# Weights that stream through the array stand 80 bytes nearer to the front of their ring places than weights that are loaded into it

## The chip, the cores and the metric

The kernel runs on one core of one Trainium2 chip. The metric is the device time of one execution in microseconds (us). TensorE (PE in the rows, PEld for its weight loads) multiplies, ScalarE (ACT) and VectorE (DVE) work elementwise, and SyncE (SP) issues the DMAs. GpSimd does nothing here.

## The reference, cut to what matters

Two layers of a decoder trunk on 256 tokens of width 2048, all in float32: a gated linear recurrence, then an attention with three branches, each followed by an MLP of width 8192 with a squared ReLU. Every sub-layer is shifted, scaled and gated by vectors that come from a condition vector and a large matrix (`ada_w`).

```
for layer in range(DEPTH):
    ...
    h = x * (1.0 + scale[:, 0, None]) + shift[:, 0, None]
    if mixer == 0: y = rglru_mixer(h, ...)      # h @ w_in, conv, gates, scan, (...) @ w_out
    elif mixer == 1: y = nsa_mixer(h, ...)      # h @ w_in, three attentions, (...) @ w_out
    x = _layer_norm(DN_ALPHA * x + (1.0 + gate[:, 0, None]) * y, ...)
    h = x * (1.0 + scale[:, 1, None]) + shift[:, 1, None]
    y = (jnp.square(jax.nn.relu(h @ w1)) @ w2)
    x = _layer_norm(DN_ALPHA * x + (1.0 + gate[:, 1, None]) * y, ...)
```

Nearly all the arithmetic is in the large products with `w_in`, `w_out`, `w1` and `w2`.

## The kernel before

**Three matmuls for one product.** A float32 operand is split into a rounded part (hi, type fp32r) and the rest (lo). `mm3` (L193 to L197) makes a product from three matmuls that add up in one PSUM bank: hi by hi (L195), hi by lo (L196), lo by hi (L197).

**The ring.** All large weights go through one stream. SP loads a unit of 128x2048 into one of six `raw` buffers (L104), ACT writes its rounded half to `whi` (L137) and DVE the rest to `wlo` (L138), 1024 columns at a time, that is two pieces of 512. `whi` and `wlo` are rings of 16 pieces; piece i lies in place i % 16, 2048 bytes a place. `pump` writes a pair of pieces only if the pair has room behind the piece that is being used (L132), and `take` (L185) moves that mark by one. The same `pump` runs the `ada` units, each a pass of DVE over 128x2048 (L120).

**Two ways to multiply.** In `gemm_ws` and `gemm_ws_outer` (L199 to L226) the weights are loaded into the array: four slices of 128 columns of a piece are loaded in turn, and 256 columns of the activations (tiles `s`) move through, so a piece takes twelve matmuls of 256 columns. In `gemm_as` (L228 to L259) a slice of 128 columns of the activations is loaded, and the whole piece of 512 columns moves through, for two halves of the tokens: six matmuls of 512 columns a piece. Rows name the moving operand last in one case and first in the other: `g<-s,whi` is a matmul of the first kind, with shape 128x256, and `g<-whi,s` one of the second, with shape 128x512.

The second kind is used for `lru_out`, for all `mlp_w2`, for two units of columns of `nsa_kv`, for `nsa_out`, and for the first 512 columns of `mlp_w1` in layer 1: 43 products of 16 pieces. Everything else is of the first kind. In the built program `whi`, `wlo` and all `s` tiles begin at multiples of 64 bytes in each partition, and so does every piece and every slice.

**The order** is that of a recorder's clock (`now`), with guessed durations (L205 to L257); the chip's own times don't enter it.

Of the kernel before, what the change touches and what calls it, by code (L numbers as in the profile page):

```python
# [10 lines left out]
F32R = mybir.dt.float32r  # L11
# [18 lines left out]

RAW = 6
RING = 16
NS4 = 20
NS2 = 6
LNACT = (0, 2)
# [5 lines left out]
class Item:  # L41
    def __init__(self, kind, src, col=None, then=None, width=2048):
        self.kind, self.src, self.col, self.then, self.width = kind, src, col, then, width
        self.group = 0
        self.done = False
        self.run = None
        self.pieces = {"w": width // 512, "g": 2}.get(kind, 0)


class Builder:  # L50
    def __init__(self, ctx, tc, a, out):
        self.tc, self.nc, self.a, self.out = tc, tc.nc, a, out
        nc = self.nc
        self.const = ctx.enter_context(tc.tile_pool(name="const", bufs=1))
        self.pool = ctx.enter_context(tc.tile_pool(name="work", bufs=1))
        self.psum = ctx.enter_context(tc.tile_pool(name="psum", bufs=1, space=PSUM))
        self.dram = ctx.enter_context(tc.tile_pool(name="dram", bufs=1, space=DRAM))
        self.raw = self.const.tile([128, RAW, 2048], F32, name="raw")
        self.whi = self.const.tile([128, RING, 512], F32R, name="whi")
        self.wlo = self.const.tile([128, RING, 512], F32R, name="wlo")  # L60
        self.now = 0.0
        self.tasks = []
        self.items = []
        self.di = self.pi = 0
        self.cons = self.prod = 0
        self.slot = self.inflight = 0
        self.arrive = []
        self.uid = 0


    def t4(self, shape, dtype=F32):
        self.uid += 1
        return self.pool.tile(shape, dtype, name=f"s{self.uid}", tag="s4", bufs=NS4)

# [11 lines left out]

    def set_stream(self, items):
        self.items = items
        p = 0
        for it in items:  # L90
            it.p0 = p
            p += it.pieces
        self.prefetch()

    def prefetch(self):
# [13 lines left out]
    def pump(self):  # L109
        nc = self.nc  # L110
        while self.pi < len(self.items):
            it = self.items[self.pi]
            if it.kind == "d":
                self.pi += 1
                continue
            if self.arrive[self.pi] > self.now:
                return
            r = it.raw
            if it.kind == "a":
                nc.vector.scalar_tensor_tensor(r, r, self.one, self.cond, op0=OP.mult, op1=OP.mult, accum_out=it.col)  # L120
            elif it.kind == "raw":
                if not it.run(r):
                    return
            elif it.kind == "p":
                it.run(r)
            elif it.kind == "n":
                if not it.done:
                    return
            else:
                w = min(1024, it.width)  # L130
                s = it.p0 + 2 * it.group
                if s + 2 > self.cons + RING:  # L132
                    return
                src = r[:, 1024 * it.group:1024 * it.group + w]
                hi = self.whi[:, s % RING:s % RING + 2, :].rearrange("p a b -> p (a b)")[:, :w]
                lo = self.wlo[:, s % RING:s % RING + 2, :].rearrange("p a b -> p (a b)")[:, :w]
                nc.scalar.activation(hi, src, AF.Copy)  # L137
                nc.vector.tensor_tensor(out=lo, in0=src, in1=hi.bitcast(F32), op=OP.subtract)  # L138
                self.prod = s + 2
                it.group += 1  # L140
                if 2 * it.group < it.pieces:
                    continue
            self.pi += 1
            self.inflight -= 1
            self.prefetch()
            if it.then:
                it.then()
# [32 lines left out]

    def piece(self, i):
        self.until(lambda: self.prod > i)
        return self.whi[:, i % RING, :], self.wlo[:, i % RING, :]

    def take(self):  # L185
        self.cons += 1

    def head(self, kind):

        self.until(lambda: self.items[self.pi].kind == kind and not self.items[self.pi].done and self.arrive[self.pi] <= self.now)  # L190
        return self.items[self.pi], self.items[self.pi].raw
# [88 lines left out]
def build(ctx, tc, a, out):  # L280
    B = Builder(ctx, tc, a, out)
# [57 lines left out]
    def W(name, *ix):  # L339
        return Item("w", a[name][ix])  # L340

    def N(name, *ix):
        return Item("n", a[name][ix])

    def merge(main, side):
        res, j = [], 0
        for i, m in enumerate(main):
            res.append(m)
            while j < len(side) and (j + 1) * len(main) <= (i + 1) * len(side):
                res.append(side[j])  # L350
                j += 1
        return res + side[j:]
# [3 lines left out]
    def hook(key):  # L356
        return lambda: hooks[key]()
# [52 lines left out]
    lru_in = [N("lru_gate", 0), N("lru_gate", 1)]  # L410
    for c in (2, 3):
        lru_in += [W("lru_in", 4 + c, g) for g in range(4)] + [W("lru_in", c, g) for g in range(4)] + [N("lru_gate", c)]
    lru_out = [W("lru_out", n, g) for n in range(4) for g in range(4)]
    def ss_group(k0, k1):
        ks = range(k0, k1)
        return ada_items(1, 0, ks) + ada_items(1, 1, ks, hook(("h1", k0, k1)))
# [9 lines left out]
    def mlp_items(l):  # L426
        its = []
        for q in range(4):
            its += [W("mlp_w1", l, 4 * q + i, g) for i in range(4) for g in range(4)]
            its += [W("mlp_w2", l, n, 4 * q + g) for n in range(4) for g in range(4)]  # L430
        return its

    m0 = mlp_items(0)
    stream += merge(m0[16:], ada_items(1, 2, then=hook(("gate", 1))) + ada_items(2, 0) + ada_items(2, 1, then=hook(("ss", 2))) + ada_items(2, 2, then=hook(("gate", 2))))
    nsa = []
    for ch in (4, 5, 0, 1, 2, 3):
        if ch == 4 or ch == 5:
            idx = {4: 3, 5: 5}[ch]
        else:
            idx = (0, 1, 2, 4)[ch]  # L440
        nsa += [W("nsa_kv", idx, g) for g in range(4)]
# [5 lines left out]
    nsa += q_items + [W("nsa_out", n, g) for n in range(4) for g in range(4)]  # L447
# [596 lines left out]
    gbank = B.bank([128, 256], "g")  # L1044
    whi, wlo = B.piece(B.cons)
    B.until(lambda: B.prod > B.cons + 1)
    ghi = B.whi[:, B.cons % RING:B.cons % RING + 2, :].rearrange("p a b -> p (a b)")
    glo = B.wlo[:, B.cons % RING:B.cons % RING + 2, :].rearrange("p a b -> p (a b)")
# [226 lines left out]
```

## Time and profile before

| | |
|---|---|
| median of 3 runs | 2256.97 us (2256.06 to 2257.09) |
| the profiled execution | 2264.49 us |
| its span, first to last instruction | 2262.7 us |
| mean granted clock of TensorE in it | 0.988 |
| PE busy | 2166.2 us (96%) |
| DVE busy | 1637.4 us (72%) |
| ACT busy | 1058.3 us (47%) |

All rows below are from the profiled execution; 1.8 us of it lie outside the span. A matmul's duration in the trace is longer than the distance to the next one, since matmuls overlap: what a matmul costs in a dense stretch is the distance from start to start, which is the length of the stretch over the count.

### The profile page before, as it was taken

The page shows a single profiled execution, that of the slowest core. Times are in us where ns is not written, and L with a number is a line of the kernel's source. Part 1 is how long each engine was busy: PE and PEld are TensorE (multiplying, and loading weights), DVE is VectorE, ACT ScalarE, POOL GpSimd, SP SyncE. Part 2 cuts the span into 40 slices and gives each one's busy share as a digit, 9 for nine tenths or more (in the row PEclk, how much of TensorE's full clock was granted, in tenths as well). Part 3 has the DMA queues.
Part 4 walks back from the last instruction along what each step waited for, and adds up shares of the span by engine and source line. Part 5 has one row for each costly group of instructions (what it writes and reads, how often), then busy time and mean ns, then how long its engine had stood idle before and what let it go on. Part 6 is the DMA issues. An engine that isn't in the chain of part 4 may idle for free.

```text
span 2262.7 us, 34098 instructions
## 1 busy us (share of the span) xinstructions
PE 2166.2 (96%) x14089; PEld 1938.8 (86%) x14089; DVE 1637.4 (72%) x1958; ACT 1058.3 (47%) x1385; POOL 0.2 (0%) x4
## 2 busy tenths in 40 slices
PE   3799998999999999999999999999999999999997
PEld 3788877998998998998789988788989989988986
DVE  8898788897777777678887688668766454454566
ACT  2356564554453454454453355536544444543541
POOL 0000000000000000000000000000000000000000
PEclk9899999999999999999999999999999999999999
DMA  9988878699878887889689875356788555555670
GB/s 392 413 328 339 348 297 344 264 355 384 334 300 307 293 326 292 302 309 341 234 298 356 301 270 214 132 200 216 284 303 320 197 186 186 189 192 196 211 255 37
DMA packets 98775, 625.02 MB, mean 276 GB/s; under 512 B 10963, under 2 KB 13443, under 8 KB 27452
## 3 DMA queue, kind: packets, MB, share of 16 engines
q1 hardware_dynamic: 98620, 622.85, 73.6%
q8 instruction: 110, 1.80, 0.3%
q14 instruction: 45, 0.37, 0.0%
HBM read 614.36 MB, written 8.45 MB: 275 GB/s over the span
## 4 chain that ended last, share of the span: by engine, by line
PE 86%; DVE 8%; ACT 3%; issue 2%; DMA 2%; SPq 0%; DVEq 0%; ACTq 0%
PE g L196 26%; PE g L195 26%; PE g L197 26%; DVE raw L120 3%; DVE wlo L138 2%; DMA raw<-in_lru_in 1%; ACT whi L137 1%; PE m L1157 1%; PE m L1123 1%; PE m L962 1%; PE m L1149 0%; PE g L873 0%; PE m L1160 0%; PE m L379 0%; DMA raw<-in_ada 0%
## 5 line engine op out<-in xcount | busy, mean ns | idle before, releaser
L138 DVE TENSOR_TENSOR wlo<-raw,whi 128x1024 fp32r<-128x1024 f32 x721 | 870.7, 1221 | 466.7 <-ACT whi L137 465.5
L137 ACT ACTIVATE whi<-raw 128x1024 fp32r<-128x1024 f32 x721 | 754.6, 1057 | 866.0 <-PE g L197 423.7
L195 PE MATMUL g<-s,whi 128*128 128x256 f32 (+1 forms) x2768 | 776.2, 281 | 58.6 <-ACT s L529 57.6
L196 PE MATMUL g<-s,whi 128*128 128x256 f32 (+1 forms) x2768 | 774.4, 280 | 3.2 <-DVE s L530 3.2
L197 PE MATMUL g<-s,wlo 128*128 128x256 f32 (+1 forms) x2768 | 773.0, 280 | 2.3 <-DVE wlo L138 2.3
L195 PEld LDWEIGHTS g<-s,whi 128*128 128x128 f32 (+1 forms) x2768 | 522.4, 189 | 72.4 <-ACT s L529 58.6
L195 PE MATMUL g<-whi,s 128*128 128x512 f32 x1376 | 542.5, 395 | 7.6 <-ACT s L529 4.2
L196 PE MATMUL g<-wlo,s 128*128 128x512 f32 x1376 | 542.1, 394 | 1.6 <-DVE wlo L138 1.6
L197 PE MATMUL g<-whi,s 128*128 128x512 f32 x1376 | 540.6, 393 | 0.3 <-DVE s L530 0.3
L197 PEld LDWEIGHTS g<-s,wlo 128*128 128x128 f32 (+1 forms) x2768 | 525.8, 190 | 6.4 <-DVE wlo L138 4.6
L196 PEld LDWEIGHTS g<-s,whi 128*128 128x128 f32 (+1 forms) x2768 | 523.2, 189 | 6.7 <-DVE s L530 4.7
L120 DVE SCALAR_TENSOR_TENSOR raw<-raw,one,cond 128x2048 f32<-128x2048 f32 x176 | 411.4, 2346 | 34.2 <-DMA raw<-in_ada 33.3
L195 PEld LDWEIGHTS g<-whi,s 128*128 128x128 f32 x1376 | 259.4, 189 | 68.0 <-ACT s L529 5.9
L196 PEld LDWEIGHTS g<-wlo,s 128*128 128x128 f32 x1376 | 259.6, 189 | 59.4 <-DVE wlo L138 2.3
L197 PEld LDWEIGHTS g<-whi,s 128*128 128x128 f32 x1376 | 259.5, 189 | 57.9 <-DVE s L530 1.8
L195 PE MATMUL m<-s,whi 128*128 128x256 f32 x256 | 70.4, 276 | 0.2 <-ACT whi L137 0.2
L197 PE MATMUL m<-s,wlo 128*128 128x256 f32 x256 | 70.6, 276 | 0.0
L196 PE MATMUL m<-s,whi 128*128 128x256 f32 x256 | 70.6, 276 | 0.0
L488 ACT ACTIVATE s<-s,hB,hA 128x256 f32<-128x256 f32 x32 | 16.7, 592 | 100.7 <-DVE hA L464 75.2
L530 DVE TENSOR_TENSOR s<-t,s 128x512 fp32r<-128x512 f32 x78 | 53.2, 684 | 4.0 <-ACT s L529 3.8
L708 ACT ACTIVATE t<-g 128x512 f32<-128x512 f32 x58 | 34.0, 587 | 34.0 <-PE g L197 34.0
L195 PEld LDWEIGHTS m<-s,whi 128*128 128x128 f32 x256 | 47.9, 188 | 0.4 <-ACT whi L137 0.4
(192 smaller groups left out, 1058.3 us busy)
## 6 DMA issues: line engine op xcount, KB each, us to landing
raw<-in_mlp_w SPq DMA_DIRECT2D x256, 1024.0 KB, 5.1
raw<-in_ada SPq DMA_DIRECT2D x176, 1024.0 KB, 7.0
raw<-in_lru_in SPq DMA_DIRECT2D x28, 1024.0 KB, 6.1
raw<-in_nsa_kv SPq DMA_DIRECT2D x24, 1024.0 KB, 5.3
raw<-in_gate SPq DMA_DIRECT2D x16, 1024.0 KB, 10.2
raw<-in_lru_out SPq DMA_DIRECT2D x16, 1024.0 KB, 7.0
raw<-in_nsa_q SPq DMA_DIRECT2D x16, 1024.0 KB, 6.6
raw<-in_nsa_out SPq DMA_DIRECT2D x16, 1024.0 KB, 4.7
```

The costliest lines, as they stand in the source:

```text
L120: nc.vector.scalar_tensor_tensor(r, r, self.one, self.cond, op0=OP.mult, op1=OP.mult, accum_out=it.col)
L137: nc.scalar.activation(hi, src, AF.Copy)
L138: nc.vector.tensor_tensor(out=lo, in0=src, in1=hi.bitcast(F32), op=OP.subtract)
L195: mm(out, lhi, rhi, start=start, stop=False, skip_group_check=True)
L196: mm(out, lhi, rlo, start=False, stop=False, skip_group_check=True)
L197: mm(out, llo, rhi, start=False, stop=stop, skip_group_check=True)
L488: SC.activation(x[:, j, :], x[:, j, :], AF.Identity, scale=hA[s][:, k:k + 1], bias=hB[s][:, k:k + 1])
L530: V.tensor_tensor(out=lo, in0=src, in1=hi.bitcast(F32), op=OP.subtract)
L708: SC.activation(r2, banks[b], AF.Relu)
L962: T.matmul(hv, r[:, 128 * l:128 * l + 128], x[:, :, h:15 + h, l], start=(h == 0 and l == 0), stop=(h == 1 and l == 15))
L1123: T.matmul(ps, qT[:, h, 128 * t:128 * t + 128], kT[g // 2][:, g % 2, :, 0:K], start=True, stop=True)
L1157: T.matmul(po, vt[br][:, kt, 128 * g:128 * g + 128], pT[:, br, kt], start=first, stop=False)
```

## The change

Pieces get an offset within their places: 64 elements (256 bytes) where they are loaded into the array, 44 elements (176 bytes) where they move through it. Both rings grow by 64 elements. A moving pair therefore reaches into the last 20 elements of the place ahead of it. Where a unit of moving pieces follows one of loaded pieces, two places of the ring are skipped; where a loaded pair would end on the first 20 elements of a moving piece that is still in use, `pump` waits for it. The units of the second kind are marked by `moving`.

```diff
+OFF_WS, OFF_AS = 64, 44
...
-        self.whi = self.const.tile([128, RING, 512], F32R, name="whi")
-        self.wlo = self.const.tile([128, RING, 512], F32R, name="wlo")
+        self.whi = self.const.tile([128, 512 * RING + 64], F32R, name="whi")
+        self.wlo = self.const.tile([128, 512 * RING + 64], F32R, name="wlo")
...
+        self.skip, self.off = set(), {}
...
+        p, last = 0, False
         for it in items:
+            if it.pieces and it.moving and not last:
+                self.skip |= {p, p + 1}
+                p += 2
             it.p0 = p
-            p += it.pieces
+            for _ in range(it.pieces):
+                self.off[p] = OFF_AS if it.moving else OFF_WS
+                p += 1
+            if it.pieces:
+                last = it.moving
...
                 if s + 2 > self.cons + RING:
                     return
+                old = s + 2 - RING
+                if not it.moving and old >= self.cons and self.off.get(old) == OFF_AS:
+                    return
...
+                o = self.off[s] + 512 * (s % RING)
+                hi, lo = self.whi[:, o:o + w], self.wlo[:, o:o + w]
...
     def take(self):
         self.cons += 1
+        while self.cons in self.skip:
+            self.cons += 1
```

In the built program the loaded pieces still begin at multiples of 64 bytes, as do the `s` tiles. The moving pieces begin 48 bytes past such a multiple.

The matmuls, their shapes and their number stay as they are. What moves is where ACT's and DVE's conversions stand among the other work, by one or two pairs. One such place is in the first layer's MLP, at the end of the second quarter of `mlp_w1`, where the ring goes over from loaded pieces to moving ones (near 650 us). `s_5347` and `s_5571` are rounded tiles of the hidden layer, `t_` their ReLUs, `g_` PSUM banks. ACT before:

```order
L137 ACTIVATE whi<-raw 128x1024 x6
L708 ACTIVATE t_5349<-g_5098 128x512
L709 ACTIVATE t_5349<-t_5349 128x512
L137 ACTIVATE whi<-raw 128x1024
L529 ACTIVATE s_5347<-t_5349 128x512
L708 ACTIVATE t_5368<-g_5099 128x512
L709 ACTIVATE t_5368<-t_5368 128x512
L137 ACTIVATE whi<-raw 128x1024
L529 ACTIVATE s_5347<-t_5368 128x512
```

And ACT at the same place after the change (lines are numbered anew: L159 is the conversion, L557 the rounding, L736 and L737 the ReLU and the square):

```order
L159 ACTIVATE whi<-raw 128x1024 x6
L736 ACTIVATE t_5349<-g_5098 128x512
L737 ACTIVATE t_5349<-t_5349 128x512
L159 ACTIVATE whi<-raw 128x1024
L557 ACTIVATE s_5347<-t_5349 128x512
L736 ACTIVATE t_5366<-g_5099 128x512
L737 ACTIVATE t_5366<-t_5366 128x512
L557 ACTIVATE s_5347<-t_5366 128x512
```

The conversion that stood ahead of the last rounding has moved behind it: the first moving pair is written one pair later. The other place is on PE, a product of `mlp_w2` in layer 0 where two output blocks of moving pieces overlap (`g_4114` and `g_4115` are the two token halves of one block, `g_4261` and `g_4262` those of the next). PE before:

```order
L195 MATMUL g_4261<-whi,s_3906 128x512
L196 MATMUL g_4261<-wlo,s_3906 128x512
L197 MATMUL g_4261<-whi,s_3907 128x512
L195 MATMUL g_4262<-whi,s_3906 128x512
L195 MATMUL g_4114<-whi,s_3983 128x512
L196 MATMUL g_4114<-wlo,s_3983 128x512
```

And after, at the same place:

```order
L220 MATMUL g_4261<-whi,s_3906 128x512
L220 MATMUL g_4262<-whi,s_3906 128x512
L221 MATMUL g_4261<-wlo,s_3906 128x512
L222 MATMUL g_4261<-whi,s_3907 128x512
L220 MATMUL g_4114<-whi,s_3983 128x512
L221 MATMUL g_4114<-wlo,s_3983 128x512
```

The same matmuls stand there, one of them two rows earlier.

## Rows read from the trace of the kernel before

**Rows 1.** The page, busy time: engine, us, share of the span, instructions.

```profile
PE 2166.2 (96%) x14089; PEld 1938.8 (86%) x14089; DVE 1637.4 (72%) x1958; ACT 1058.3 (47%) x1385; POOL 0.2 (0%) x4
```

**Rows 2.** The page, chain of work that ended last, by engine and line.

```profile
PE 86%; DVE 8%; ACT 3%; issue 2%; DMA 2%; SPq 0%; DVEq 0%; ACTq 0%
PE g L196 26%; PE g L195 26%; PE g L197 26%; DVE raw L120 3%; DVE wlo L138 2%; DMA raw<-in_lru_in 1%; ACT whi L137 1%; PE m L1157 1%; PE m L1123 1%; PE m L962 1%; PE m L1149 0%; PE g L873 0%; PE m L1160 0%; PE m L379 0%; DMA raw<-in_ada 0%
```

**Rows 3.** Groups by line and form: count, busy us, mean ns, idle before.

```profile
L195 PE MATMUL g<-s,whi 128*128 128x256 f32 x2752 | 771.7, 281 | 58.6 <-ACT s L529 57.6 <-ACT whi L137 1.1
L195 PE MATMUL g<-whi,s 128*128 128x512 f32 x1376 | 542.5, 395 | 7.6 <-ACT s L529 4.2 <-ACT whi L137 3.4
L195 PE MATMUL m<-s,whi 128*128 128x256 f32 x256 | 70.4, 276 | 0.2 <-ACT whi L137 0.2
```

**Rows 4.** PE in dense stretches of moving pieces: window, PE busy (count), granted clock, DMA.

```profile
500.00:580.00 80.00, 80.00 (x352) 1.00 0.95 377
680.00:755.00 75.00, 75.00 (x323) 1.00 0.83 308
1815.00:1890.00 75.00, 75.00 (x330) 1.00 0.55 190
2170.00:2245.00 75.00, 75.00 (x330) 1.00 0.30 106
```

**Rows 5.** The same view in dense stretches of loaded pieces.

```profile
590.00:628.00 38.00, 38.00 (x338) 1.00 0.87 334
634.00:670.00 36.00, 36.00 (x308) 1.00 0.77 291
1565.00:1625.00 60.00, 60.00 (x512) 1.00 0.82 291
1720.00:1805.00 85.00, 85.00 (x725) 1.00 0.65 236
1900.00:1985.00 85.00, 85.00 (x724) 1.00 0.55 186
2080.00:2160.00 80.00, 80.00 (x709) 1.00 0.65 223
```

**Rows 6.** Groups by form in the window 1815 to 1890 us.

```profile
L196 PE MATMUL g<-wlo,s 128*128 128x512 f32 x110 | 43.3, 394 | 0.0
L195 PE MATMUL g<-whi,s 128*128 128x512 f32 x110 | 43.1, 392 | 0.0
L197 PE MATMUL g<-whi,s 128*128 128x512 f32 x110 | 42.7, 388 | 0.0
```

**Rows 7.** Timeline of PE, the gate products: start us, length, line, tiles, shape, count.

```profile
225.65 1.89 PE L873 MATMUL m<-s,raw 128*128 128x256 f32 x8
227.37 1.89 PE L873 MATMUL g<-s,raw 128*128 128x256 f32 x8
229.10 1.89 PE L873 MATMUL m<-s,raw 128*128 128x256 f32 x8
```

**Rows 8.** Waits: who waited for whom, total us, times, longest.

```profile
ACT whi L137 <- PE g L197: 423.7, 256, 11.3
ACT whi L137 <- PE g L196: 364.8, 223, 5.2
...
PEld g L195 <- ACT whi L137: 7.3, 4, 4.3
...
PEld g L197 <- DVE wlo L138: 4.6, 4, 1.5
```

**Rows 9.** Groups by line and form, the conversions.

```profile
L138 DVE TENSOR_TENSOR wlo<-raw,whi 128x1024 fp32r<-128x1024 f32 x720 | 869.8, 1222 | 466.1 <-ACT whi L137 465.0
...
L137 ACT ACTIVATE whi<-raw 128x1024 fp32r<-128x1024 f32 x720 | 753.7, 1057 | 865.6 <-PE g L197 423.7 <-PE g L196 364.4 <-DMA raw<-in_lru_in 23.5
```

More of the change, by code (lines that the diff above doesn't have):

```diff
@@ L47, in __init__, with moving @@
         self.pieces = {"w": width // 512, "g": 2}.get(kind, 0)
+        self.moving = False
+def moving(items):
+    for it in items:
+        it.moving = True
+    return items
 class Builder:
@@ L88, in set_stream @@
         self.items = items
-        p = 0
+        p, last = 0, False
         for it in items:
+            if it.pieces and it.moving and not last:
+                self.skip |= {p, p + 1}
+                p += 2
             it.p0 = p
-            p += it.pieces
+            for _ in range(it.pieces):
[3 more added lines that the diff above has]
+                last = it.moving
         self.prefetch()
@@ L133, in pump @@
                     return
+                old = s + 2 - RING
+                if not it.moving and old >= self.cons and self.off.get(old) == OFF_AS:
+                    return
                 src = r[:, 1024 * it.group:1024 * it.group + w]
-                hi = self.whi[:, s % RING:s % RING + 2, :].rearrange("p a b -> p (a b)")[:, :w]
-                lo = self.wlo[:, s % RING:s % RING + 2, :].rearrange("p a b -> p (a b)")[:, :w]
+                o = self.off[s] + 512 * (s % RING)
+                hi, lo = self.whi[:, o:o + w], self.wlo[:, o:o + w]
                 nc.scalar.activation(hi, src, AF.Copy)
@@ L182, in piece @@
         self.until(lambda: self.prod > i)
-        return self.whi[:, i % RING, :], self.wlo[:, i % RING, :]
+        o = self.off[i] + 512 * (i % RING)
+        return self.whi[:, o:o + 512], self.wlo[:, o:o + 512]
     def take(self):
         self.cons += 1
+        while self.cons in self.skip:
+            self.cons += 1
     def head(self, kind):
@@ L412, in build @@
         lru_in += [W("lru_in", 4 + c, g) for g in range(4)] + [W("lru_in", c, g) for g in range(4)] + [N("lru_gate", c)]
-    lru_out = [W("lru_out", n, g) for n in range(4) for g in range(4)]
+    lru_out = moving([W("lru_out", n, g) for n in range(4) for g in range(4)])
     def ss_group(k0, k1):
@@ L429, in mlp_items @@
             its += [W("mlp_w1", l, 4 * q + i, g) for i in range(4) for g in range(4)]
-            its += [W("mlp_w2", l, n, 4 * q + g) for n in range(4) for g in range(4)]
+            its += moving([W("mlp_w2", l, n, 4 * q + g) for n in range(4) for g in range(4)])
+        if l == 1:
+            moving(its[:4])
         return its
@@ L440, in build @@
             idx = (0, 1, 2, 4)[ch]
-        nsa += [W("nsa_kv", idx, g) for g in range(4)]
+        its = [W("nsa_kv", idx, g) for g in range(4)]
+        nsa += moving(its) if ch in (4, 5) else its
     nsa.append(Item("g", a["nsa_g"], width=768))
@@ L446, in build @@
         nsa.insert(at, cmp_raw[i])
-    nsa += q_items + [W("nsa_out", n, g) for n in range(4) for g in range(4)]
+    nsa += q_items + moving([W("nsa_out", n, g) for n in range(4) for g in range(4)])
     stream += merge(nsa, ada_items(3, 0) + ada_items(3, 1, then=hook(("ss", 3))))
@@ L1046, in build @@
     B.until(lambda: B.prod > B.cons + 1)
-    ghi = B.whi[:, B.cons % RING:B.cons % RING + 2, :].rearrange("p a b -> p (a b)")
-    glo = B.wlo[:, B.cons % RING:B.cons % RING + 2, :].rearrange("p a b -> p (a b)")
+    go = OFF_WS + 512 * (B.cons % RING)
+    ghi, glo = B.whi[:, go:go + 1024], B.wlo[:, go:go + 1024]
     for k in range(NK):
```

## The prediction

> **What bounds the kernel now.** I read the page first, busy times and then the chain. PE is busy for 96% of the span and DVE for 72% [rows 1]; 86% of the chain that ended last is PE, and 78% is the three matmul lines of `mm3` [rows 2]. So a nanosecond on each matmul counts nearly in full, and a stall of DVE or ACT counts only where it reaches PE.
>
> Next I asked what one matmul costs. Durations mislead, since matmuls overlap (a mean of 395 ns for the moving kind [rows 3]), so I took dense stretches in which PE has no gap and divided their length by the count. A matmul that hangs over the edge of a window is counted too, so the length gets one duration added: 0.39 us for the moving kind, 0.28 us for the loaded kind.
>
> Moving pieces (512 columns): 80.39/352 = 228.4 ns, 75.39/330 = 228.5 ns twice, and in one stretch 75.39/323 = 233.4 ns [rows 4]. I read ten such windows over the whole span; nine gave 228 to 229 ns and that one 233.4, so the mean is 228.9 ns. The granted clock is 1.00, the full 2.4 GHz, in all of them, and the DMA share goes from 0.30 to 0.95 without a trace in the spacing.
>
> Loaded pieces (256 columns): 38.28/338 = 113.2 ns and 80.28/709 = 113.2 ns in some stretches, 36.28/308 = 117.8, 60.28/512 = 117.7, 85.28/725 = 117.6 and 85.28/724 = 117.8 ns in others [rows 5], again at full clock. Of nine such windows five are at 113.2 to 113.5 and four at 117.6 to 117.8.
>
> Two things are to be seen here. The spacing takes few values and holds one of them for tens of microseconds, on the same code and the same addresses, and load on DVE or the DMA queues doesn't go with it. That looks like a matter of phase between two regular streams, and the two that PE always has are the operand that moves and the slice that is being loaded for the next matmul. And within one dense stretch of moving pieces the three lines of `mm3` have three different mean durations, 392, 394 and 388 ns, 110 matmuls each [rows 6]: same shape, same clock, no waits. What differs between the three lines is which slice is loaded while which piece moves. So something in how the two meet costs up to 6 ns a matmul, and it could depend on their relative place in memory. In the kernel before, all of them lie at multiples of 64 bytes, so the trace holds no second case to compare.
>
> **What the change does, part by part.**
>
> *The offset of moving pieces.* It touches the second kind alone: 1376 matmuls on each of three lines, 4128 in all [rows 3]. The trace doesn't show a moving piece at another place, so I bound the new spacing.
>
> From below: the closest that 512 column slots stand in any row is the gate products at L873, plain float32 with 256 columns a record, eight records in 227.37 - 225.65 = 1.72 us and 229.10 - 227.37 = 1.73 us, which is 216 ns each [rows 7]. They are another type and another line, so this is a far bound: (228.9 - 216) x 4128 = 53 us less.
>
> From above: 233.4 ns is the slowest state that moving pieces show over a whole stretch [rows 4]: (233.4 - 228.9) x 4128 = 19 us more.
>
> Between them the nearest row is the loaded kind in its better state: same type, same two streams, 113.2 ns for 256 columns, so 226.4 ns for 512 [rows 5]. The 388 ns line of rows 6, the shortest of the three, says the same: one of the three matmuls already runs without the extra few nanoseconds. I take 226.4 ns for all of them: (228.9 - 226.4) x 4128 = 10.3 us less.
>
> The Trainium skill, page "TensorE: Matmul & The Clock Gate", section "Back-to-back issue gap", gives N/2.4 + 2.5 ns for a matmul of N columns at full clock, 215.8 ns for 512. No stretch of the moving kind here comes near it; by that figure the sum could be 54 us less, which is about the far bound that the gate products give.
>
> *Loaded pieces.* They move by 256 bytes and the `s` tiles by 512; relative to each other and to 64 bytes nothing visible changes. Taken at nothing. What it costs if that is wrong: a loaded matmul between its two states is 4.5 ns, four windows hold 2269 matmuls in the worse one (308 + 512 + 725 + 724), of 9024 in all (2752 + 256 on each of three lines [rows 3]). If those all came back, 10 us less; if the other 6755 slipped, 30 us more.
>
> *The skipped places.* Ten times the stream goes from loaded to moving pieces, and two of 16 places stand empty for a while; nine times it goes back, and a loaded pair waits for one more `take`. The ring then reaches 14 pieces ahead, 14 x 12 x 113.2 ns = 19 us of PE's work, not 16 pieces and 22 us. In the order, one pair's conversion moves behind one rounding (the two fences of ACT). ACT's longest waits are for PE to free a place, 424 and 365 us in total, while PE waited for `whi` four times, 7.3 us in all, and for `wlo` four times, 4.6 us [rows 8]: the conversions are ahead. So this costs nothing, and the cover is that 19 us. Were it gone, a pair is 1.06 us on ACT and then 1.22 us on DVE [rows 9], 2.3 us a transition and at most 19 x 2.3 = 43 us; I see nothing that would uncover it, since a pair occupies PE for 2.7 us and the slower engine for 1.2.
>
> SP issues the same units, each at most two pieces of work later. The matmul that stands two rows earlier on PE (the second order) is one of equal cost between neighbours of equal cost: nothing.
>
> *The conversions themselves* write to places that begin at 176 bytes and no longer at a multiple of 64. ACT takes 1057 ns and DVE 1222 ns a pair [rows 9]. Even 10% more on the moving ones (344 pairs, 0.12 us) would be 41 us of DVE in work that runs ahead of PE: nothing on the path.
>
> **The sum.** The profiled execution took 2264.5 us (span 2262.7 and 1.8 around it), 7.5 us above the median of the runs. 2264.5 - 10.3 = 2254.2 for a profiled execution, and with the same 7.5 us off, 2246.7 for the median.
>
> **The rivals.**
>
> *A, forecast: the moving kind falls to 226.4 ns.* About 2247, and 2241 to 2252.5 with the remainder of the bound on the loaded stretches. For it: the unequal lines of rows 6 and the two states. Against: one value of offset, and no row at another.
>
> *B, more: the moving kind falls below 226 ns.* Half way to the gate products, 222 ns, is 28 us less, 2229; the whole way is 2204. For it: float32 at the same number of slots runs at 216 ns with the same slices being loaded. Against: loaded pieces never go below 113.2 ns in nine windows, so half of the excess looks like part of the type.
>
> *C, nothing.* The place of an operand makes no difference to PE, and the unequal lines come from elsewhere, such as PSUM or the order of issue. Then the spacing stays at 228.9, the ring costs nothing and the time stays within 4.5 us of 2257. For it: the two states come and go at unchanged addresses, so the address is not all of it. The Trainium skill, page "SBUF — State Buffer", section "Who interferes with whom", gives PE two independent read ports, one for the moving operand and one for weight loads, and says that PE never waits on anyone; by that rule this rival holds. The trace so far neither bears that out nor refutes it.
>
> *D, slower: the offset puts the moving kind in its worse state for good.* 233.4 ns in all stretches is 19 us more, 2276; it decides from 1.1 ns a matmul on (4.5/4128), a spacing of 230.0. For it: that state exists and held for the whole of a stretch [rows 4]; a piece that begins 48 bytes past a multiple of 64 may need one more access at its ends. Against: nine windows of ten are in the other state at present.
>
> *E, slower by the loaded stretches.* They follow moving stretches and could inherit another phase; with a quarter of the 6755 in the worse state, 7.6 us more, 2265.
>
> **How the numbers follow.** A 0.36, B 0.24, C 0.17, D 0.15, E 0.08. A measurement of this kernel can tell about 0.2%, 4.5 us, from no change: faster is A and B, 0.60; same is C, 0.17; slower is D and E, 0.23. The likeliest gives 2247. The range must reach into B and D: from 2208, which leaves out the last part of B, to 2276, which holds D's price and leaves out what lies beyond it. A's own range is 2241 to 2252.5.
>
> **What would show it.** In dense stretches of moving pieces, 80 us should hold 355 matmuls where it held 352 (80.39/226.4), and the three lines should have one mean duration near 388 ns. Stretches of loaded pieces should count as before, about 709 in 80 us or 724 in 85. PE's waits for `whi` and `wlo` should stay near 7 and 5 us. B would show 360 or more in 80 us; C 352 with the same unequal lines; D 345 and lines near 397 ns; E more stretches at 117.7. I am wrong if the time moves while the spacing of moving pieces does not, or if PE's wait for conversions grows by more than some microseconds.

## The result and the profile after: slower by 1.2%

The changed kernel takes 2284.4 us (median of 4 runs, 2282.7 to 2287.2), the kernel before 2257.0 us beside it (2256.1 to 2258.8): a ratio of 1.0116, 95% interval 1.0103 to 1.0129. The forecast was 2247, the range ended at 2276. The profiled execution took 2287.2 us with a span of 2285.5, which is 22.8 us more than the span before.

The page of the changed kernel, busy times and conversions (L159 and L160 are now the conversions, L220 to L222 are `mm3`):

```profile
PE 2189.7 (96%) x14089; PEld 1944.1 (85%) x14089; DVE 1638.6 (72%) x1958; ACT 1059.4 (46%) x1385; POOL 0.2 (0%) x4
...
L160 DVE TENSOR_TENSOR wlo<-raw,whi 128x1024 fp32r<-128x1024 f32 x721 | 870.4, 1222 | 474.0 <-ACT whi L159 470.1
L159 ACT ACTIVATE whi<-raw 128x1024 fp32r<-128x1024 f32 x721 | 754.6, 1057 | 889.1 <-PE g L222 441.6
...
L220 PE MATMUL g<-whi,s 128*128 128x512 f32 x1376 | 553.7, 403 | 7.3 <-ACT s L557 4.0
```

PE is busy 23.5 us longer with the same 14089 instructions, while DVE's and ACT's busy times moved by about 1 us [rows 1]. The conversions cost what they cost [rows 9]. The moving matmuls of the first line of `mm3` grew from 395 ns [rows 3] to 403 ns.

The windows in dense stretches of moving pieces, which answer to [rows 4] (window, PE busy with its count, granted clock, DMA share, GB/s):

```profile
505.00:585.00 80.00, 80.00 (x339) 1.00 0.95 363
685.00:765.00 80.00, 80.00 (x339) 1.00 0.83 310
1835.00:1910.00 75.00, 75.00 (x319) 1.00 0.53 183
2185.00:2260.00 75.00, 75.00 (x319) 1.00 0.39 139
```

75.40/319 = 236.4 ns, and 80.40/339 = 237.2 ns, where it was 228.5 (by single starts both stand at 236.7). The clock is the full 2.4 GHz here too. 75 us hold 319 matmuls instead of 330. The groups by form in the window 1835 to 1910 us answer to [rows 6]:

```profile
L220 PE MATMUL g<-whi,s 128*128 128x512 f32 x107 | 42.8, 400 | 0.0
L222 PE MATMUL g<-whi,s 128*128 128x512 f32 x106 | 42.4, 400 | 0.0
L221 PE MATMUL g<-wlo,s 128*128 128x512 f32 x106 | 42.4, 400 | 0.0
```

All three lines stand at 400 ns. None of them waits. The windows in loaded stretches, beside [rows 5]:

```profile
600.00:638.00 38.00, 38.00 (x337) 1.00 0.88 337
640.00:675.00 35.00, 35.00 (x300) 1.00 0.70 266
1588.00:1645.00 57.00, 57.00 (x505) 1.00 0.78 274
1745.00:1820.00 75.00, 75.00 (x665) 1.00 0.68 244
1925.00:2000.00 75.00, 75.00 (x664) 1.00 0.54 185
2100.00:2175.00 75.00, 75.00 (x665) 1.00 0.64 220
```

75.28/665 = 113.2 ns and 35.28/300 = 117.6 ns: the same two values, but the stretches at 1588, 1745 and 1925 us, which stood at 117.7 before, now stand at 113.3. And the waits of PE's weight loads for the conversions, beside [rows 8]:

```profile
PEld g L220 <- ACT whi L159: 7.5, 4, 4.3
PEld g L222 <- DVE wlo L160: 4.2, 4, 1.5
```

They are unchanged within 0.4 us. To size the two kinds over the whole program I took the distance from start to start of neighbouring matmuls of one kind wherever no gap lies between them (98% of all): the moving kind went from 229.41 to 236.44 ns, the loaded kind from 114.75 to 114.07. So the moving kind gave 7.03 x 4128 = +29.0 us, the loaded kind -0.68 x 9024 = -6.1 us, together +22.9 of the 22.8 us by which the span grew. These two terms suffice for the two profiled executions. That they meet the span to 0.1 us is partly luck: the same sum misses the growth of the span by 5 us in as48 and by 7 us in ws44 (both below). By the medians the time grew by 27.4 us, since the profiled execution of the kernel before was 7.5 us above its median and that of the changed kernel 2.8. The same means are used for the experiments below.

### The profile page after: what moved, and what is told of

It reads as the page before. It is cut to its first block, busy times and chain, and to the rows that moved or that the text cites. A ratio compares the mean times of both kernels' runs of the same rounds, so it can differ in the third digit from the quotient of the medians.

```text
span 2285.5 us, 34079 instructions
## 1 busy us (share of the span) xinstructions
PE 2189.7 (96%) x14089; PEld 1944.1 (85%) x14089; DVE 1638.6 (72%) x1958; ACT 1059.4 (46%) x1385; POOL 0.2 (0%) x4
## 4 chain that ended last, share of the span: by engine, by line
PE 86%; DVE 8%; ACT 2%; issue 2%; DMA 1%; SPq 0%; DVEq 0%; ACTq 0%
PE g L220 26%; PE g L222 26%; PE g L221 26%; DVE raw L139 3%; DVE wlo L160 2%; PE m L1185 1%; PE m L1151 1%; ACT whi L159 1%; DMA raw<-in_ada 1%; DMA raw<-in_lru_in 1%; PE m L990 1%; PE m L220 1%; PE m L221 0%; PE m L222 0%; PE g L901 0%
## 5 line engine op out<-in xcount | busy, mean ns | idle before, releaser
L160 DVE TENSOR_TENSOR wlo<-raw,whi 128x1024 fp32r<-128x1024 f32 x721 | 870.4, 1222 | 474.0 <-ACT whi L159 470.1
L159 ACT ACTIVATE whi<-raw 128x1024 fp32r<-128x1024 f32 x721 | 754.6, 1057 | 889.1 <-PE g L222 441.6
L220 PE MATMUL g<-s,whi 128*128 128x256 f32 (+1 forms) x2768 | 774.3, 281 | 58.7 <-ACT s L557 57.5
L222 PE MATMUL g<-s,wlo 128*128 128x256 f32 (+1 forms) x2768 | 770.3, 279 | 1.9 <-DVE wlo L160 1.8
L220 PEld LDWEIGHTS g<-s,whi 128*128 128x128 f32 (+1 forms) x2768 | 522.9, 189 | 72.9 <-ACT s L557 58.3
L220 PE MATMUL g<-whi,s 128*128 128x512 f32 x1376 | 553.7, 403 | 7.3 <-ACT s L557 4.0
L221 PE MATMUL g<-wlo,s 128*128 128x512 f32 x1376 | 552.6, 402 | 2.1 <-DVE wlo L160 2.1
L222 PE MATMUL g<-whi,s 128*128 128x512 f32 x1376 | 551.7, 402 | 0.3 <-DVE s L558 0.3
L222 PEld LDWEIGHTS g<-s,wlo 128*128 128x128 f32 (+1 forms) x2768 | 522.7, 189 | 6.1 <-DVE wlo L160 4.2
L220 PEld LDWEIGHTS g<-whi,s 128*128 128x128 f32 x1376 | 262.6, 191 | 73.0 <-ACT s L557 5.6
L222 PEld LDWEIGHTS g<-whi,s 128*128 128x128 f32 x1376 | 263.0, 191 | 65.8 <-DVE s L558 2.0
L220 PE MATMUL m<-s,whi 128*128 128x256 f32 x256 | 71.2, 280 | 0.2 <-ACT whi L159 0.2
L222 PE MATMUL m<-s,wlo 128*128 128x256 f32 x256 | 71.1, 278 | 0.0
L736 ACT ACTIVATE t<-g 128x512 f32<-128x512 f32 x58 | 33.9, 587 | 33.0 <-PE g L222 33.0
L220 PEld LDWEIGHTS m<-s,whi 128*128 128x128 f32 x256 | 48.5, 190 | 0.4 <-ACT whi L159 0.4
```

The costliest lines, as they stand in the source:

```text
L220: mm(out, lhi, rhi, start=start, stop=False, skip_group_check=True)
L221: mm(out, lhi, rlo, start=False, stop=False, skip_group_check=True)
L222: mm(out, llo, rhi, start=False, stop=stop, skip_group_check=True)
L736: SC.activation(r2, banks[b], AF.Relu)
```

## The experiments

What was open: is it the offset or the ring's machinery; is it the absolute place of a piece or its place relative to the other operand; and why do several spacings exist at one place? The kernels of the table compute the whole model; the three maps are blocks of matmuls alone and leave the transformer out. The ratio is to the kernel before in the same batch of runs on the same chip, where its median was 2257.0 to 2261.1 us; so the ratios compare, and the medians of different rows only roughly.

| kernel | offset loaded, moving (elements) | moving ns | loaded ns | median us | ratio, interval |
|---|---|---|---|---|---|
| before | 0, 0 | 229.41 | 114.75 | 2257.0 | |
| the change | 64, 44 | 236.44 | 114.07 | 2284.4 | 1.0116 [1.0103, 1.0129] |
| as0 | 64, 0 | 229.39 | 114.03 | 2262.3 | 1.0005 [0.9982, 1.0027] |
| as48 | 64, 48 | 226.93 | 116.32 | 2268.7 | 1.0035 [1.0019, 1.0051] |
| ws44 | 44, 44 | 232.85 | 118.52 | 2306.3 | 1.0194 [1.0168, 1.0221] |
| nudge44 | 64, 44 | 236.2 | 113.7 | 2294.1 | 1.0159 [1.0142, 1.0176] |
| turn44_72 | 64, 44 | 234.9 | 113.9 | 2287.1 | 1.0126 [1.0111, 1.0142] |
| turn44_70 | 64, 44 | 236.3 | 114.0 | 2286.1 | 1.0124 [1.0110, 1.0137] |
| turn48_72 | 64, 48 | 226.9 | 116.6 | 2271.9 | 1.0057 [1.0044, 1.0070] |
| turn48_64 | 64, 48 | 226.9 | 116.4 | 2269.8 | 1.0049 [1.0035, 1.0063] |
| tail64 | 64, 48 and 64 | 227.34 | 114.77 | 2253.3 | 0.9975 [0.9962, 0.9987] |

**as0: the machinery without the offset.**

```diff
-OFF_WS, OFF_AS = 64, 44
+OFF_WS, OFF_AS = 64, 0
```

> The changed kernel with the moving pieces 256 bytes nearer to the front and not 80, so at multiples of 64 bytes again; skipped places, waits and order as in the change. OWN and DISTANCE: spacing of the moving kind back to 229 ns and the time back to about 2257 us (2250 to 2268, the state of the loaded stretches being free). RING: the time stays near 2284.

Its span is 2256.0 us and its moving kind stands at 229.39 ns, as before. Skipped places and the extra wait of `pump` are all still there, and cost nothing that can be measured (the interval ends at 6 us). The 29 us on the moving kind are the offset's; RING falls.

**as48: the moving pieces 16 bytes further.**

```diff
-OFF_WS, OFF_AS = 64, 44
+OFF_WS, OFF_AS = 64, 48
```

> The changed kernel with moving pieces 64 bytes nearer to the front. OWN: 229 ns and about 2257 us. DISTANCE modulo 64 bytes: the same. DISTANCE modulo 256 bytes: another spacing than 229, in either direction, 10 us or more from 2257. RING: near 2284.

Windows of as48, two in moving stretches and two in loaded ones:

```profile
505.00:580.00 75.00, 75.00 (x333) 1.00 0.96 378
1825.00:1900.00 75.00, 75.00 (x332) 1.00 0.56 190
590.00:670.00 80.00, 80.00 (x681) 1.00 0.79 298
770.00:850.00 80.00, 80.00 (x682) 1.00 0.80 299
```

75.39/333 = 226.4 ns: the spacing that I had forecast, at an offset 16 bytes from the one in the change, and all three lines of `mm3` last 389 ns there:

```profile
L221 PE MATMUL g<-wlo,s 128*128 128x512 f32 x111 | 43.2, 389 | 0.0
L222 PE MATMUL g<-whi,s 128*128 128x512 f32 x111 | 43.2, 389 | 0.0
L220 PE MATMUL g<-whi,s 128*128 128x512 f32 x110 | 42.8, 389 | 0.0
```

OWN and DISTANCE modulo 64 bytes, which both gave 229 ns, fall. But 80.28/682 = 117.7 ns in the loaded stretches: each of the seven that follow a moving stretch at once (from 587, 765, 943, 1178, 1727, 1904 and 2082 us) stands in the worse of its two states from its start to its end. About two thirds of all loaded matmuls do, against three in ten before. Against the kernel before the moving kind gives -10.2 us and the loaded kind +14.2. The span grew by 9.1 us; the 5 us beyond the sum lie mostly ahead of 500 us, where stretches have gaps, and I did not trace them further.

**ws44: both kinds shifted alike.** The offsets are 44 and 44, and `pump` asks the old piece's kind, no longer its offset.

```diff
-OFF_WS, OFF_AS = 64, 44
+OFF_WS, OFF_AS = 44, 44
...
-                if not it.moving and old >= self.cons and self.off.get(old) == OFF_AS:
+                if not it.moving and old >= self.cons and self.mov.get(old):
```

> The changed kernel with the loaded pieces too at 176 bytes, so that all pieces of the ring lie 48 bytes past a multiple of 64; the activations stay at multiples of 64. OWN: moving kind as after the change (236.6 ns), loaded kind as before (113.3 or 117.8 ns), time near 2284 us. DISTANCE: the moving kind as after the change, and the loaded kind changes its spacing too, by 2 ns or more a matmul, 18 us or more in the time. RING: near 2284 with spacings as after the change.

Windows of ws44, two moving and two loaded:

```profile
690.00:765.00 75.00, 75.00 (x318) 1.00 0.84 312
870.00:945.00 75.00, 75.00 (x332) 1.00 0.82 307
780.00:855.00 75.00, 75.00 (x642) 1.00 0.79 293
960.00:1035.00 75.00, 75.00 (x627) 1.00 0.80 291
```

The moving pieces lie where the change puts them within their places, yet one stretch has 75.40/318 = 237.1 ns and another 75.39/332 = 227.1. The loaded pieces, whose only shift is against the `s` tiles, now have 117.3 and 120.1 ns. So the loaded kind, too, changes its spacing with the place of its slices, as DISTANCE said. And one layout has more than one spacing, which neither OWN nor DISTANCE had foreseen.

**map1: where the two operands lie.** Blocks of 48 matmuls each; the moving operand, the loaded one or both are shifted in steps of 16 bytes, with whi, wlo and the activations at the same places modulo 256 bytes as in the kernel.

```python
    for r in "xy":
        for i in range(16):
            moving(f"m{LET[i]}{r}", 4 * i, 0)
            if r == "y":
                spacer()
    for i in range(16):
        moving(f"l{LET[i]}x", 0, 4 * i)
    for i in range(16):
        moving(f"b{LET[i]}x", 4 * i, 4 * i)
...
```

The first number is the shift of the moving piece in elements, the second that of the loaded slice; `spacer` is a transpose.

> Not the reference's work: a row of dense blocks of 48 matmuls on one piece of weights and one tile of activations, each block with another offset, 16 bytes a step from 0 to 240 bytes, and nothing else running. Blocks m: moving 512 columns offset, loaded slice at a multiple of 64 bytes (twice, the second time with a transpose between blocks). Blocks l: loaded slice offset, moving at a multiple of 64. Blocks b: both by the same offset. Blocks u: moving by 4, 8, 12 and 256 bytes. Blocks n: 256 moving columns offset; blocks k: the loaded slice of these offset. OWN (a moving operand off a multiple of 64 bytes costs by itself): m at 0, 64, 128, 192 bytes near 229 ns, all other m near 236.6; l all 229; b as m. DISTANCE (what counts is how moving and loaded operand stand to each other, modulo 64 bytes): m as under OWN or a ramp over the 16 byte steps, l mirrors m, and b is 229 everywhere. RING (conversions and their order make the difference, not the offset): all blocks near 229.

Blocks of map1, one tile's view each (name, count, duration shortest/median/longest, first to last start): both operands at 0, then the moving one at 44 elements in the first and in the second pass, then at 48, then the loaded one at 20 and the moving one at 0.

```profile
L55 PE MATMUL bax<-whi,shi x16: 394/394/394, 549.1 to 559.4; 128*128 128x512 f32 x16
L55 PE MATMUL mlx<-whi,shi x16: 388/388/396, 136.0 to 146.2; 128*128 128x512 f32 x16
L56 PE MATMUL mly<-wlo,shi x16: 393/398/403, 315.3 to 326.0; 128*128 128x512 f32 x16
L55 PE MATMUL mmx<-whi,shi x16: 389/389/397, 146.9 to 157.1; 128*128 128x512 f32 x16
L55 PE MATMUL lfx<-whi,shi x16: 389/389/389, 426.5 to 436.7; 128*128 128x512 f32 x16
```

From first to last start there are 45 matmuls: 10.3/45 = 229 ns, 10.2/45 = 227, 10.7/45 = 238, 10.2/45 = 227, 10.2/45 = 227. By single starts the blocks settle at 228.9, 226.7, 236.7, 226.7 and 226.7. With both operands shifted alike the sixteen blocks settle at 228.9 or 226.7 ns and never at more; with the moving one alone shifted, most have 229 to 235 ns, of its sixteen places only 44 and 48 elements reach 226.7, and 44 has 226.7 in one pass and 236.7 in the other. With the loaded one alone shifted, only 16 and 20 elements reach 226.7: the same two distances from the moving operand to the loaded one, 48 and 44, counted modulo 64 elements (256 bytes). That is the case for a relative place, and for several patterns at one place. Steps finer than 16 bytes count too: at 4 and 8 bytes the moving kind has 234.8 and 235.5 ns.

**map2: what comes ahead of a block.** Pairs of a loaded and a moving block, with a plain float32 matmul of no, 64, 65, ... 79 columns between them.

> Not the reference's work: dense blocks as in the first map, each pair a change from one kind to the other, with one short float32 matmul of 64 to 79 columns (or none) between the two. ha then hw: moving pieces at 192 bytes (48 elements), then loaded pieces; qw then qa: loaded, then moving at 176 bytes (44 elements, as in the change); rw then ra: loaded, then moving at 192; ta then tw: moving at 0, then loaded; vw then va: loaded, then moving at 0. ONE (an offset has one spacing): within each set all blocks of a kind have the same spacing, qa 236.6, ra 226.7, va 228.9, hw and tw 113.3. PHASE (an offset allows several regular patterns, and the instant at which a block begins picks one): within a set the spacing changes with the length of the matmul between, qa between 226.7 and 236.6 and perhaps others, hw between 113.3 and 117.8, and it stays the same to the end of a block.

Blocks of map2: moving at 44 directly behind a loaded block, the same behind 70 columns; then loaded behind a moving block at 48, directly and behind 65 columns.

```profile
L56 PE MATMUL qaa<-wlo,shi x16: 392/400/403, 207.3 to 217.9; 128*128 128x512 f32 x16
L56 PE MATMUL qah<-wlo,shi x16: 388/388/389, 307.3 to 317.5; 128*128 128x512 f32 x16
L65 PE MATMUL hwa<-slo,whi x16: 281/281/282, 20.9 to 26.2; 128*128 128x256 f32 x16
L65 PE MATMUL hwc<-slo,whi x16: 276/276/282, 42.8 to 47.9; 128*128 128x256 f32 x16
```

By single starts: 236.7 and 226.7 ns, 117.8 and 113.4 ns. At 44 two of the 17 entries (70 and 72 columns) give 226.7, one 233.3, the others 236.7; at 48 all settle at 226.7. Loaded blocks directly behind one at 48 stand at 117.8 (18 of 18), those directly behind one at 0 at 113.3 (17 of 17). The pattern is also handed on: moving blocks at 0 directly behind a loaded one at 117.8 stand at 233.3 (14 of 14), behind one at 113.3 at 228.9 (3 of 3). So how a block is entered picks among its patterns, and it keeps the one picked. ONE falls. One entry isn't what its name says: the 64-column matmul of set h ran at 13.6 us, 18 us ahead of all but the first matmul of its loaded block, which was entered directly and stands at 117.8.

**nudge44, turn44_72, turn44_70, turn48_72, turn48_64: steering by what comes ahead.** A plain float32 matmul of 64 columns ahead of every moving product (nudge44), or of 72 or 70 ahead of the moving stretches only (turn44), or of 72 or 64 ahead of the loaded ones (turn48). The edit for moving stretches:

```diff
+    def turn(self, kind, bank):
+        n = {"ws": None, "as": 72}[kind]
+        if self.last != kind and n:
+            self.nc.tensor.matmul(bank[:, 0:n], self.ident, self.ident[:, 0:n], start=True, stop=True, skip_group_check=True)
+        self.last = kind
```

> The changed kernel with one extra float32 matmul of 64 columns ahead of each of the 43 products of the moving kind (its result is overwritten), some 0.12 us each, 5 us in all; offset of 176 bytes kept. ONE: moving kind at 236.6 ns all over, time 5 us above the changed kernel, about 2289. PHASE: some of the 43 products at 226.7 ns and others at 236.6, each for its whole length; with half of them better, 20 us less and 5 more, about 2269.

> The changed kernel as it is (offsets 64 and 44), with a plain fp32 matmul of 72 columns issued ahead of the first matmul of a moving stretch wherever the product before it was of the loaded kind. In the second map such a block of 72 columns turned the 44-offset from 236.7 to 226.7 ns; 64 columns left it at 236.7. PHASE (an offset admits several patterns and the instant at which a stretch begins picks one): 4128 moving matmuls at 226.7 instead of 236.4 ns, -40 us, about 2244 us if every stretch turns, and between 2244 and 2284 us by the share of stretches that turn. ONE PATTERN (236.6 ns belongs to the offset): moving matmuls stay at 236.4 ns and the time is that of the change, 2284 to 2286 us.

> The same with 70 columns, which also gave 226.7 ns at offset 44 in the second map. PHASE: as with 72 columns, about 2244 us if every stretch turns, and the same stretches need not turn as with 72. ONE PATTERN: 2284 to 2286 us.

> Offset 48 for the moving pieces, and a plain fp32 matmul of 72 columns ahead of the first matmul of a loaded stretch wherever the product before it was of the moving kind. Without it offset 48 gave 226.9 ns moving and 116.3 ns loaded (two thirds of the loaded matmuls at 117.8). In the second map 72 columns there brought the loaded matmuls from 117.8 to 113.3 ns. PHASE: moving stays at 226.9 ns (-10 us against the kernel before), loaded falls to 113.3 to 114 ns (-7 to -13 us against it), together about 2235 to 2242 us, faster than both kernels. ONE PATTERN: what a loaded stretch takes does not hang on its start, loaded stays at 116.3 ns, about 2265 us as with offset 48 alone.

> The same with 64 columns, the control: in the second map 64 columns left the loaded matmuls at 117.8 ns. PHASE: no gain over offset 48 alone, about 2265 us, with loaded near 116.3 ns. If any matmul put in between does it, whatever its length: about 2240 us as with 72 columns.

As a lever this failed all four times: nudge44, turn44_72, turn44_70 and turn48_72 came nowhere near the time that PHASE gave them, and only turn44_72 brought a stretch to 226.7 ns. turn48_64, meant as the control, gained nothing, as expected; but the block of map2 on which it rests had been entered directly, so it says little of 64 columns. nudge44 stays at 236.2 ns, which is what map2 says of 64 columns at 44, and pays for 43 matmuls more. Two windows of turn44_72:

```profile
505.00:580.00 75.00, 75.00 (x333) 1.00 0.98 380
680.00:760.00 80.00, 80.00 (x340) 1.00 0.83 307
```

The stretch at 500 us stands at 75.39/333 = 226.4 ns from its start to its end, 10 ns below its value in the changed kernel, at the same offset; the next one at 80.40/340 = 236.5. Two more, from 304 and from 1482 us, stand at 233.3, and the other long ones at 236.7. So ONE PATTERN is refuted in the whole kernel too. But PHASE in the form in which I had put it, that the number of columns ahead picks the pattern, did not carry over: in turn48_72 the loaded stretches stay at 117.8 ns behind 72 columns (80 us hold 682), although the first starts lie 62, 76 and 201 ns apart there, to the nanosecond as in the block of map2 that turned behind 72 columns.

**map3: is there a place at which the loaded kind is always good?** Loaded blocks at 16 shifts, behind a moving block at 48, entered in five ways.

> Blocks alone, no transformer: each time 24 moving matmuls at offset 48, then 48 loaded ones whose slices of the ring are shifted by 0, 16, ... 240 bytes, entered in five ways: directly, after a plain fp32 matmul of 70 or of 72 columns, after a transpose, and with a transpose in the middle. PHASE (an offset admits several patterns and the start picks one): at shift 0 the five entries give both 113.3 and 117.8 ns; other shifts have patterns of their own, and if one shift gives 113.3 ns whatever the entry, the loaded pieces belong there, and a kernel with it and moving pieces at 48 takes about 2235 to 2240 us. ONE PATTERN (a shift fixes the spacing): the five entries agree at each shift, as in the first map: 113.3 ns at shifts 0 and 128 bytes, 116.7 to 120 ns at the others.

Blocks of map3: shift 0 entered directly and behind 72 columns, then a shift of 144 bytes entered directly.

```profile
L65 PE MATMUL waa<-slo,whi x16: 281/281/281, 20.4 to 25.7; 128*128 128x256 f32 x16
L65 PE MATMUL wac<-slo,whi x16: 276/276/282, 42.3 to 47.4; 128*128 128x256 f32 x16
L65 PE MATMUL wja<-slo,whi x16: 276/278/279, 578.8 to 584.0; 128*128 128x256 f32 x16
```

By single starts 117.8, 113.4 and 116.7 ns. Shifts of 0 and 128 bytes have both 113.3 and 117.8, depending on the entry; 144 and 160 bytes have 116.7 in every entry; the others stand at 117.3 to 120.0. No shift is good whatever comes ahead. (map1 has 113.3 ns also with the activations, which move here, shifted by 176 bytes, in the one block that has it; no run tried that further.) The two at which the good pattern exists are the multiples of 128 bytes, and loaded pieces lie there already.

**tail64: leave the moving stretch by another pattern.** The offset is 48, but the last product ahead of a change to loaded pieces lies at 64, which is where 0 is, modulo 256 bytes.

```diff
-OFF_WS, OFF_AS = 64, 44
+OFF_WS, OFF_AS = 64, 48
...
+        fed = [it for it in items if it.pieces]
+        tail = {id(x) for i, y in enumerate(fed) if i and fed[i - 1].moving and not y.moving for x in fed[i - 4:i]}
...
-                self.off[p] = OFF_AS if it.moving else OFF_WS
+                self.off[p] = OFF_AS if it.moving and id(it) not in tail else OFF_WS
...
-                if not it.moving and old >= self.cons and self.off.get(old) == OFF_AS:
+                if self.off[s] == OFF_WS and old >= self.cons and self.off.get(old) == OFF_AS:
```

> Offset 48 for the moving pieces except those of the last product ahead of a change to the loaded kind, which lie at 64 (256 bytes, where a moving product took 228.9 to 229.4 ns in the kernel before). With all moving pieces at 48 every loaded stretch that followed one directly stood at 117.8 ns; behind moving pieces at 0 it mostly stood at 113.4 ns. START (how the last moving product leaves the array picks the pattern of the loaded stretch behind it): loaded falls from 116.3 to 113.4 to 114.5 ns, -16 to -26 us against offset 48 alone, while about a tenth to a quarter of the moving matmuls pay 2 ns more (+1 to +2 us): about 2243 to 2255 us beside 2259 us for the kernel before, faster than it by 0.2 to 0.7%. PRESENCE (some pieces at 48 anywhere in the ring slow the loaded kind): loaded stays at 116.3 ns, 2268 to 2272 us.

Windows of tail64: a moving stretch and its last product, then loaded stretches.

```profile
500.00:560.00 60.00, 60.00 (x267) 1.00 0.98 372
562.00:580.00 18.00, 18.00 (x80) 1.00 0.95 368
590.00:625.00 35.00, 35.00 (x311) 1.00 0.90 350
765.00:840.00 75.00, 75.00 (x664) 1.00 0.82 301
...
1895.00:1970.00 75.00, 75.00 (x664) 1.00 0.55 191
2070.00:2150.00 80.00, 80.00 (x682) 1.00 0.62 210
```

60.39/267 = 226.2 ns up to the last product, 18.39/80 = 229.9 in it, and then 35.28/311 = 113.4 and 75.28/664 = 113.4 ns in the loaded stretch. Of the seven loaded stretches that follow at once, six enter at 113.3 (none in as48, five in the kernel before); the last, from 2064 us, stands at 117.7. So START holds and PRESENCE falls.

The last stretch can be told from the others by what ended ahead of it. Its moving product has the same mean spacing as the other six, but within the round of three matmuls another one is the short one. The product that ends at 584 us, then the one that ends at 2064 us, by lines:

```profile
L222 PE MATMUL g<-whi,s 128*128 128x512 f32 x29 | 11.4, 394 | 0.0
L224 PE MATMUL g<-whi,s 128*128 128x512 f32 x29 | 11.4, 392 | 0.0
L223 PE MATMUL g<-wlo,s 128*128 128x512 f32 x29 | 11.3, 388 | 0.0
...
L223 PE MATMUL g<-wlo,s 128*128 128x512 f32 x26 | 10.2, 394 | 0.0
L222 PE MATMUL g<-whi,s 128*128 128x512 f32 x26 | 10.2, 392 | 0.0
L224 PE MATMUL g<-whi,s 128*128 128x512 f32 x26 | 10.1, 388 | 0.0
```

With the third line short, the first loaded matmul starts 226 ns behind the last moving one; with the second short, 236 ns. The kernel before agrees: the stretch of [rows 6] has its third line short and hands over to the loaded stretch from 1897 us, which is at 117.8 [rows 5]. In the eight whole-model kernels whose loaded pieces lie at multiples of 256 bytes and have no short matmul put ahead of them, all 56 direct entries fit: 225 to 227 ns ten times, each time 117.8; 230 to 242 ns 46 times, each time 113.3. That is a regularity and not a shown cause, and one entry of map2 breaks it (227 ns, then 113.4).

The loaded mean is 114.77, as before (START had given 113.4 to 114.5), and the moving mean 2.07 ns lower: -8.5 us, and the span is 2254.3, 8.4 less than before. It is the fastest kernel here, by 0.25% of the kernel before (interval 0.13 to 0.38%), 1.4% ahead of the change.

## Why the prediction was wrong

**What bounds the kernel: right.** The two spacings account for the 22.8 us between the profiled executions, so the method, spacing times count, held. Also right was the suspicion that the relative place of the moving and the loaded operand is at work, in patterns that hold for tens of microseconds: as0 against the change shows the place, ws44 and map1 that it is relative, map2 and turn44_72 the several patterns.

**The step that failed: "I take 226.4 ns for all of them".** It should have been -10.3 us and was +29.0. Two moves led there. I took the better state of the loaded kind as the floor of the moving kind, which it is (226.7 in as48 and map1), and then let the change reach that floor, for which no row spoke: nothing in the trace says that 48 bytes past a multiple of 64 is the place of the floor. 16 bytes further on, in as48, the moving kind does stand at that floor. Nor did the short line of [rows 6] speak for it: in the stretch from 500 to 580 us of the same kernel it is L195 that has the 388 ns, so the short one is a place in a repeating round of three and not a line that is free of the extra. And I bounded it from above by 233.4, the slowest state that the trace showed. A state seen at one offset doesn't bound another offset: at 44 the chip has 226.7, 233.3 and 236.7, and in the changed kernel nearly all matmuls are in the last. With that bound the range could not hold the result.

**Rival D was right in its direction and mis-sized.** It said that the offset puts the moving kind in a worse state for good; its price was 4.5 ns and 19 us, measured 7.0 ns and 29.0 us, of which in the profiled executions the loaded kind gave back 6.1. Its sign to look for, 345 matmuls in 80 us and lines near 397 ns, came as 339 and 400. Its reason, one more access at the ends of a piece that begins off a multiple of 64 bytes, isn't borne out: pieces at 44 elements also stand at 226.7 ns in a block of map1 and in stretches of ws44.

**Rival C falls** on as0 and the change, which differ only in the moving pieces' offset and by 7 ns on each moving matmul. The Trainium skill, page "SBUF — State Buffer", section "Who interferes with whom", says that PE never waits on anyone; in map1 the moving kind goes from 226.7 to 236.7 ns with both operands long in place and nothing else running, which that rule doesn't lead one to expect. Whether the read ports are what does it, no run here shows. B falls too: no kernel and no block has a mean of the moving kind below 226.6 ns.

**Loaded pieces, taken at nothing:** -6.1 us, within the bound of 10 that I gave. It isn't the moving offset's doing: as0 has the same 114.03 ns. Which stretches stand in the worse state differs from one trace to the next, and there is one trace for each kernel. In the kernel before it is the stretch from 1565 us, entered after a pause, and the two that inherit from it, some 9 us of its profiled execution, which was 7.5 us above the median. So the 6.1 us may belong to that execution more than to the change; this is not shown. E named the right mechanism, a pattern inherited from the moving stretch ahead, and as48 is its case, with two thirds of the loaded matmuls in the worse state.

**The skipped places and the conversions, nothing:** right. as0 has all of them at 1.0005, PE's waits for `whi` and `wlo` went from 7.3 and 4.6 to 7.5 and 4.2 us, and a pair still takes 1057 and 1222 ns.

**What stays open.** What in the chip makes the patterns was not measured; the experiments only tell where operands lie, what ran ahead, and the spacing that followed. That the product ahead picks the pattern of a loaded stretch is shown by tail64 against as48 in six cases of seven. The seventh goes with the order within the round of three, which no run set on purpose; what sets that order, and what picks the pattern of a moving stretch at 44, is not settled.

## What to carry to other kernels

Where PE's matmuls stand back to back, measure their spacing from start to start and compare it with the least that any stretch of that shape shows: if whole stretches sit a few per cent above it, at full clock and with no wait, try the relative place of the two operands in steps of 16 bytes in a small block kernel before arguing which is best, since neighbours can be 10 ns apart. A state seen in one layout doesn't bound what another layout can cost. And judge a layout by the stretches behind it too: at 48 the moving kind won 10 us, the loaded stretches behind it gave them all back, and moving only the last product won them again.

## What the hardware showed that I had not expected

One layout has several stable patterns, and a stretch holds the one with which it begins: at an offset of 44 elements 226.7, 233.3 and 236.7 ns, in loaded stretches 113.3 and 117.8. Where a stretch changes in its middle, as the loaded one from 590 to 670 us does before [rows 5] and after, a gap or another matmul stands there (in this one a transpose at 631.5 us, `m<-ident`); without one, and at one offset, no stretch of the eleven whole-model kernels went over to another spacing for good.

These values lie on a grid. Three matmuls in a row take 340.0, 353.3, 680.0, 686.7 and 700.0 ns, and six of the slowest pattern 1420 ns (236.7 each): all multiples of 6.667 ns, which is 16 cycles at 2.4 GHz. The least that any run showed is 113.3 ns for 256 columns and 226.7 for 512, which at 2.4 GHz is 17 cycles for 16 columns. Why, no run shows. The Trainium skill, page "TensorE: Matmul & The Clock Gate", section "Back-to-back issue gap", gives N/2.4 + 2.5 ns, 215.8 for 512 columns, and calls it the gap of an isolated matmul; no stretch of the moving kind came nearer to it than 226.7.
